# Unequal strides for the activation tiles of a float32 decoder trunk on one core

## The chip, the cores and the metric

The kernel runs on one core of a Trainium2 chip. The metric is the device time of one execution in microseconds, the median of several runs. One execution is profiled by the hardware profiler; its rows are what this text reads. Engines are named as in the profile: PE is TensorE (PEld its weight loads), DVE VectorE, ACT ScalarE, POOL GpSimd, SP SyncE.

## What is computed

A decoder trunk of two layers on 512 tokens of width 1024, in float32. Each layer adds half a SwiGLU, a mixer and another half SwiGLU, each on an RMSNorm of x:

```
h = _rmsnorm(x, ffn_pre_norm[l])
x = x + 0.5 * _swiglu(h, ffn_pre_w_gate[l], ffn_pre_w_up[l], ffn_pre_w_down[l])
h = _rmsnorm(x, mix_norm[l])
x = x + mixer(h)          # layer 0: retention | dilated attention; layer 1: gated linear attention
h = _rmsnorm(x, ffn_post_norm[l])
x = x + 0.5 * _swiglu(h, ffn_post_w_gate[l], ffn_post_w_up[l], ffn_post_w_down[l])
...
def _swiglu(h, wg, wu, wd):
    return (jax.nn.silu(h @ wg) * (h @ wu)) @ wd
```

The hidden width of the SwiGLU is 2816 = 22 x 128. A final RMSNorm ends the trunk.

## The kernel before

x stands transposed in SBUF, as eight tiles of 128 features x 512 tokens. Every float32 product is made of three products of halves (mm3, L121 to L126): a tensor is split into hi, a copy in fp32r, and lo, the rest. `mm3` multiplies hi weights by hi activations (L124), hi weights by lo activations (L125) and lo weights by hi activations (L126), all into the same PSUM bank. In each the weight slice, 128 x 128, is the stationary operand and the activation tile, 128 x 512, the moving one. In proj_n_steps (L249) it is the other way round: slices of the normed tile are stationary and the weights move.

**The normed tiles.** scaled (L165) makes xgh on ACT and xgl on DVE from x[k] and a gain, eight of each, from the pool xg with eight buffers for each tag (2048 bytes per partition and buffer). They are read by all projections of a stage; the row scale of the norm is applied to the products later.

**The SwiGLU tiles.** ffn (L292) computes 22 tiles of silu(gate) * up; halves (L112) splits each into acth and actl, from a pool with 22 buffers for each. For gate and up, 44 projections of 8 x 3 products run (proj_steps, L230); then eight output tiles of 22 x 3 products each (down, L330). There are four such stages, and the very last output tile is computed in two halves of 256 tokens (last_half, L338). halves also makes the tiles of cat, the mixers' outputs, which out_steps (L266) multiplies.

**The weights.** load_w (L83) loads a raw tile of up to 128 x 1024 on the SP queue and splits it on ACT (L89) and DVE (L90) into whi and wlo, four buffers of 4096 bytes each; weights (L77) keeps three tiles ahead of the one in use.

**Where tiles lie.** A pool is a stretch of the partition, opened in the order const, keep, xg, wpool, misc, and behind them the pool of the stage (ffn, even or odd). Within a pool each tag has its buffers one behind another. xg takes 16 x 2048 bytes, wpool 2 x 4096 for the raw tiles and 8 x 4096 for the halves. misc holds 14 KiB in tiles of 2048 bytes and small tiles which, with their alignment, take 448 bytes. So the ffn pool begins 448 bytes past a multiple of 512 from the weights. A weight slice is 512 bytes long, and the slices of a tile follow each other.

**The norm's row.** rows (L205) turns a column of values by token into a row in all partitions. For each of two halves DVE writes diag, a 128 x 512 tile (L215), and PE multiplies it by ones (L217), both into one PSUM bank; diag has two buffers. rows is called by stats_rows (L224) for the six norms with a weight behind them, by norm_steps (L403) for the eight heads of the mixers and by last_half for the two halves of the final norm:

```
for i in range(2):
    diag = self.t2k(self.misc, "diag", F32R, bufs=2)
    nc.vector.tensor_tensor(out=split2(diag[:, :nt * P]), ...)
    nc.tensor.matmul(ps[:, :nt * P], lhsT=self.ones_r, rhs=diag[:, :nt * P], start=i == 0, stop=i == 1)
```

**The order.** Each engine works through its instructions in a fixed order. It is planned when the program is built: of the instructions of an engine whose operands and buffers the planner expects to be ready, the one written first goes first. The steps of a norm are put off by hook (L93) to the ends of later projections, or to two places within a down tile; in the mixers, fill and weave (L99, L107) write projections between the steps of the heads. A tile's buffer is given to the next tile of its tag when the last reader is done.

Of the kernel before, what the change touches and what calls it, by code (L numbers as in the profile page):

```python
# [13 lines left out]
F32R = mybir.dt.float32r  # L14
# [3 lines left out]
PSUM = bass.MemoryType.PSUM  # L18

P = 128  # L20
T = 512
# [8 lines left out]
HELD = 4  # L30
PASS3 = 0.65
DOWN_SPLIT = ((0, 8), (8, 15), (15, 22))

# [12 lines left out]
class Trunk:  # L46
# [15 lines left out]
    @contextmanager  # L62
    def banks(self, **tags):
        """The PSUM banks of a phase, by purpose."""
        with self.tc.tile_pool(name=self.uid("ps"), bufs=1, space=PSUM, reuse_waits="tile") as self.ps:
            self.tags = tags
            yield
# [7 lines left out]

# [1 line left out]
    def weights(self):  # L77
        """The next weights of the plan, in halves."""
        while self.plan and len(self.ready) <= LOOK:
            self.ready.append(self.load_w(*self.plan.pop(0)))  # L80
        return self.ready.pop(0)
# [11 lines left out]
    def hook(self):  # L93
        """One of the steps put off, if any."""
        if self.pending:
            with self.tc.issue_after(self.last):
                self.pending.pop(0)()

    def fill(self, filler, us):  # L99
        """Of the filler, about this much work for the tensor engine."""  # L100
        while us > 0:
            t = next(filler, None)
            if t is None:
                return
            us -= t
# [4 lines left out]

# [1 line left out]
    def halves(self, pool, tag, src, bufs):  # L112
        """src (an SBUF or PSUM tile) as two parts of 12 significant bits each."""
        nc = self.nc
        hi = self.t2k(pool, tag + "h", F32R, bufs)
        lo = self.t2k(pool, tag + "l", F32R, bufs)
        nc.scalar.copy(out=hi, in_=src)  # L117
        nc.vector.tensor_tensor(out=lo, in0=src, in1=hi.bitcast(F32), op=ALU.subtract)  # L118
        return hi, lo

    def mm3(self, out, w, x, first, last):  # L121
        """out += w.T @ x with (hi, lo) pairs."""
        mm = self.nc.tensor.matmul
        mm(out, lhsT=w[0], rhs=x[0], start=first, stop=False)  # L124
        mm(out, lhsT=w[0], rhs=x[1], start=False, stop=False)  # L125
        self.last = mm(out, lhsT=w[1], rhs=x[0], start=False, stop=last).ins  # L126

# [1 line left out]
    def setup(self):  # L129
# [33 lines left out]

# [1 line left out]
    def scaled(self, k, idx):  # L165
        """gain * x[k] in halves."""
        nc = self.nc
        g = self.gain[:, idx * KD + k: idx * KD + k + 1]
        hi = self.t2k(self.xg, "xgh", F32R)
        lo = self.t2k(self.xg, "xgl", F32R)  # L170
        nc.scalar.activation(out=hi, in_=self.x[k], func=AF.Copy, scale=g)
        nc.vector.scalar_tensor_tensor(out=lo, in0=self.x[k], scalar=g, in1=hi.bitcast(F32), op0=ALU.mult, op1=ALU.subtract)
        if k == 0:
            self.h = []
        self.h.append((hi, lo))

    def prep(self, k, idx):
        """From x[k]: gain * x in halves, and the squares into their sum."""
        self.scaled(k, idx)
        self.squares(k)  # L180
# [13 lines left out]
    def rstd_cols(self, cols, parts, n, out, nt=NT):  # L194
        """cols: PSUM [P, nt]; sums over the partitions of parts, by token; out = (mean + eps)^-0.5."""
        nc = self.nc
        for t in range(nt):
            for i, p in enumerate(parts):
                nc.tensor.matmul(cols[:, t:t + 1], lhsT=p[:, t * P:(t + 1) * P], rhs=self.ones[:, 0:1],  # L199
                                 start=i == 0, stop=i == len(parts) - 1)  # L200
        v = self.t2k(self.misc, "var", bufs=2, shape=[P, NT])
        nc.vector.tensor_scalar(out=v[:, :nt], in0=cols[:, 0:nt], scalar1=1.0 / n, scalar2=EPS, op0=ALU.mult, op1=ALU.add)
        nc.gpsimd.tensor_tensor(out=out[:, :nt], in0=v[:, :nt], in1=self.mhalf[:, 0:nt], op=ALU.pow)

    def rows(self, cols, tag, nt=NT):  # L205
        """[P, nt] values by token -> PSUM [P, nt * P], the same row in every partition, by exact halves."""
        nc = self.nc
        ps = self.psum(tag)
        half = self.t2k(self.misc, "colh", F32R, bufs=2, shape=[P, 2, NT])
        ident = self.ident.unsqueeze(1).broadcast_to([P, nt, P])  # L210
        nc.vector.tensor_copy(out=half[:, 0, :nt], in_=cols[:, :nt])
        nc.vector.tensor_tensor(out=half[:, 1, :nt], in0=cols[:, :nt], in1=half[:, 0, :nt].bitcast(F32), op=ALU.subtract)
        for i in range(2):
            diag = self.t2k(self.misc, "diag", F32R, bufs=2)
            nc.vector.tensor_tensor(out=split2(diag[:, :nt * P]), in0=ident, in1=half[:, i, :nt].bitcast(F32).unsqueeze(2).broadcast_to([P, nt, P]),  # L215
                                    op=ALU.mult)
            nc.tensor.matmul(ps[:, :nt * P], lhsT=self.ones_r, rhs=diag[:, :nt * P], start=i == 0, stop=i == 1)  # L217
        return ps
# [9 lines left out]

# [1 line left out]
    def proj_steps(self, done):  # L230
        """One 128-wide tile of outputs, transposed: PSUM [outputs, tokens], before the row scale."""
        w = self.weights()
        ps = self.psum("pj")
        for k in range(KD):
            s = slice(k * P, (k + 1) * P)
            self.mm3(ps, (w[0][:, s], w[1][:, s]), self.h[k], k == 0, k == KD - 1)
            if k < KD - 1:
                yield PASS3
        done(ps)
        yield PASS3  # L240
# [8 lines left out]
    def proj_n_steps(self, tags, done):  # L249
        """512 outputs, tokens on partitions: 4 PSUM tiles, before the row scale."""  # L250
        ps = [self.psum(t) for t in tags]
# [14 lines left out]
    def out_steps(self, order, early, tags, idx):  # L266
        """The mixer's output projection; the first tiles wait with the last of cat."""
        nc = self.nc
# [21 lines left out]

# [1 line left out]
    def ffn(self, nxt):  # L292
        nc, tc = self.nc, self.tc
        with tc.tile_pool(name=self.uid("ffn"), bufs=KF, reuse_waits="tile") as pool, self.banks(pj=6, sc=2):
            act, held = [], []

            def glu(g, u):
# [5 lines left out]
                nc.vector.tensor_tensor(out=us, in0=us, in1=gs, op=ALU.mult)  # L303
                act.append(self.halves(pool, "act", us, KF))

# [32 lines left out]
    def last_half(self, d, ws, act, ts):  # L338
        """The end of the trunk for half of the tokens: the last tile of x, the final norm, the output."""
        nc = self.nc  # L340
# [25 lines left out]

# [1 line left out]
    def rotate(self, pool, ps, cos, sin, out, shift):  # L368
        """out = ps * cos + (ps with its rotary halves exchanged) * sin."""
        nc = self.nc  # L370
# [19 lines left out]
    def centered(self, pool, ps, t, width):  # L390
        """v * rstd less its mean over each head's width, from one PSUM tile of proj_n."""
        nc = self.nc
# [10 lines left out]
    def norm_steps(self, pool, outs, gates, cat, sq_tag, sq_bufs):  # L403
        """outs: PSUM tiles [e, tokens] of one head, with zero mean over e; cat: their index in cat."""
        nc = self.nc
# [174 lines left out]
    def retention(self, pool, qk, v, gates, need, more):  # L580
        """Emits all but the end of the last head's norm, which it returns."""
        nc = self.nc
# [37 lines left out]

# [1 line left out]
    def mixer_odd(self, nxt):  # L622
# [3 lines left out]
        with tc.tile_pool(name="odd", bufs=1, reuse_waits="tile") as pool, self.banks(pj=3, sc=3, o=2):  # L626
# [26 lines left out]
            def cums(h):  # L653
# [6 lines left out]
                nc.scalar.activation(out=e2, in_=b, func=AF.Exp, scale=-1.0)  # L660
                # In the place of the column that is exp(0), the first half's decay came.
                mid, end = slice(P // 2 - 1, T, P), slice(P - 1, T, P)
# [45 lines left out]
    def gla(self, pool, h, q, k, v, ex, tri, gates):  # L708
# [8 lines left out]
        for c in range(NT):  # L717
            nc.tensor.matmul(sc[:, sl[c]], lhsT=k[:, sl[c]], rhs=q[:, sl[c]], start=True, stop=True)
        # Of the upper right quarter of each block nothing is read: its exponents may be out of range.
        st = self.t2k(pool, "st", bufs=2)  # L720
# [72 lines left out]
def constants():  # L793
    """Tables that follow from the shapes alone."""
    f32 = np.float32
# [33 lines left out]
def layout(x, ffn_pre_norm, ffn_pre_w_gate, ffn_pre_w_up, ffn_pre_w_down, mix_norm, ab_w_in, ab_w_out, gla_w_in, gla_w_a2,  # L829
           gla_b_a, gla_w_out, ffn_post_norm, ffn_post_w_gate, ffn_post_w_up, ffn_post_w_down, final_norm):  # L830
    def tiles(w):
        """[K, N] -> [N/128, 128 (K within), K/128 * 128 (N within)]"""
        k, n = w.shape
        return w.reshape(k // P, P, n // P, P).transpose(2, 1, 0, 3).reshape(n // P, P, k)

    def wide(w):
        """[1024, 512] -> [4, 128 (K within), 2 * 512]"""
        return w.reshape(KD // 2, 2, P, T).transpose(0, 2, 1, 3).reshape(KD // 2, P, 2 * T)
# [39 lines left out]
```

## Time and profile before

| | |
|---|---|
| Runs, us | 1982.97 (median), 1982.41, 1985.41 |
| Profiled execution, first to last instruction, us | 1979.8 |
| PE busy | 1962.6 us, 99% |
| DVE, ACT, POOL busy | 45%, 31%, 5% |
| HBM read | 179.89 MB, 92 GB/s over the span |

The page gives the profiled execution by its span; a run's time also holds what lies around the span. The busy time of PE is the sum of its records; a record goes from the start of a product to its modelled end, and the next product starts before that. The time from one product's start to the next is read from the timeline, whose first column is the start in microseconds from the span's begin.

### The profile page before, as it was taken

How to read it: one execution, taken by the hardware profiler on the slowest of the kernel's cores; microseconds unless marked ns; L12 is line 12 of the kernel's file. 1: busy time of each engine (PE TensorE's matmuls, PEld its weight loads, DVE VectorE, ACT ScalarE, POOL GpSimd, SP SyncE). 2: the span in 40 equal slices, each digit the busy share in tenths (PEclk: the TensorE clock that was granted, in tenths of full speed). 3: DMA queues.
4: the chain of work that ended last, by engine and by line, in shares of the span. 5: the costliest groups of instructions: out<-in, count | busy, mean ns of one | idle time of the engine just before them, and what ended most of it. 6: DMA issues, size and time to landing. Idle time of an engine off the chain costs nothing.

```text
span 1979.8 us, 21475 instructions
## 1 busy us (share of the span) xinstructions
PE 1962.6 (99%) x8822; PEld 1593.8 (81%) x8822; DVE 900.2 (45%) x1238; ACT 611.9 (31%) x813; POOL 96.7 (5%) x69
## 2 busy tenths in 40 slices
PE   8999999999999999999999999999999999999998
PEld 7888888877777888888888888888788888888887
DVE  6444433444565544443334444333456564444323
ACT  5332222233332332222223323222424243323221
POOL 1000001100001200000110000011000020000010
PEclk9999999999999999999999999999999999999999
DMA  5333222421121322333332323323222133322222
GB/s 172 96 96 96 94 97 89 139 77 63 54 70 49 117 96 96 96 95 97 95 98 96 96 96 96 92 95 101 92 78 72 54 117 96 96 96 95 97 88 72
DMA packets 54548, 183.38 MB, mean 93 GB/s; under 512 B 6177, under 2 KB 8481, under 8 KB 54450
## 3 DMA queue, kind: packets, MB, share of 16 engines
q1 hardware_dynamic: 51408, 177.76, 28.0%
q10 hardware_dynamic: 3042, 4.26, 0.7%
q8 instruction: 69, 1.13, 0.2%
q14 instruction: 29, 0.24, 0.0%
HBM read 179.89 MB, written 2.10 MB: 92 GB/s over the span
## 4 chain that ended last, share of the span: by engine, by line
PE 98%; issue 0%; DVE 0%; DMA 0%; POOL 0%; ACT 0%; POOLq 0%; DVEq 0%; SPq 0%
PE pj L124 31%; PE pj L126 30%; PE pj L125 30%; PE sc L519 1%; PE o L547 1%; PE sc L199 1%; PE sc L594 0%; PE tp L535 0%; PE sc L217 0%; PE o L751 0%; PE o L744 0%; PE sc L733 0%; DMA wraw<-in_w_gu 0%; PE tp L603 0%; PE o L124 0%
## 5 line engine op out<-in xcount | busy, mean ns | idle before, releaser
L89 ACT CAST whi<-wraw 128x1024 fp32r<-128x1024 f32 (+1 forms) x341 | 352.0, 1033 | 1125.8 <-PE pj L125 669.0
L124 PE MATMUL pj<-xgh,whi 128*128 128x512 f32 x1704 | 677.6, 398 | 6.9 <-ACT whi L89 6.9
L126 PE MATMUL pj<-xgh,wlo 128*128 128x512 f32 x1704 | 664.9, 390 | 0.0
L125 PE MATMUL pj<-xgl,whi 128*128 128x512 f32 x1704 | 664.7, 390 | 0.0
L90 DVE TENSOR_TENSOR wlo<-wraw,whi 128x1024 fp32r<-128x1024 f32 (+1 forms) x341 | 413.1, 1212 | 306.1 <-ACT whi L89 305.0
L124 PEld LDWEIGHTS pj<-xgh,whi 128*128 128x128 f32 x1704 | 320.6, 188 | 83.5 <-issue 12.1
L126 PEld LDWEIGHTS pj<-xgh,wlo 128*128 128x128 f32 x1704 | 320.4, 188 | 67.9 <-DVE wlo L90 0.8
L125 PEld LDWEIGHTS pj<-xgl,whi 128*128 128x128 f32 x1704 | 320.9, 188 | 63.9 <-issue 1.0
L124 PE MATMUL pj<-acth,whi 128*128 128x512 f32 (+1 forms) x726 | 281.0, 387 | 0.0
L126 PE MATMUL pj<-acth,wlo 128*128 128x512 f32 (+1 forms) x726 | 280.9, 387 | 0.0
L125 PE MATMUL pj<-actl,whi 128*128 128x512 f32 (+1 forms) x726 | 280.9, 387 | 0.0
L302 DVE TENSOR_TENSOR us<-pj,rrow 128x512 f32<-128x512 f32 x88 | 60.8, 691 | 272.3 <-PE pj L126 272.3
L126 PEld LDWEIGHTS pj<-acth,wlo 128*128 128x128 f32 x726 | 135.8, 187 | 31.8
L125 PEld LDWEIGHTS pj<-actl,whi 128*128 128x128 f32 x726 | 135.8, 187 | 31.6
L124 PEld LDWEIGHTS pj<-acth,whi 128*128 128x128 f32 x726 | 135.8, 187 | 31.5
L189 POOL TENSOR_TENSOR sqa<-sqa,sq 128x512 f32<-128x512 f32 x41 | 70.6, 1722 | 1426.7 <-issue 798.1
L300 DVE TENSOR_TENSOR gs<-pj,rrow 128x512 f32<-128x512 f32 x88 | 60.8, 691 | 173.7 <-PE pj L126 173.7
L117 ACT CAST acth<-us 128x512 fp32r<-128x512 f32 x88 | 55.0, 625 | 61.1 <-DVE us L303 61.1
L303 DVE TENSOR_TENSOR us<-us,gs 128x512 f32<-128x512 f32 x88 | 60.9, 693 | 9.4 <-ACT gs L301 0.8
L325 DVE SCALAR_TENSOR_TENSOR x<-pj,x 128x512 f32<-128x512 f32 x31 | 21.5, 693 | 93.0 <-PE pj L126 93.0
L118 DVE TENSOR_TENSOR actl<-us,acth 128x512 fp32r<-128x512 f32 x88 | 60.4, 686 | 4.9 <-ACT acth L117 4.8
L301 ACT ACTIVATE gs<-gs 128x512 f32<-128x512 f32 x88 | 55.3, 630 | 4.2 <-DVE gs L300 4.2
(164 smaller groups left out, 1172.2 us busy)
## 6 DMA issues: line engine op xcount, KB each, us to landing
wraw<-in_w_gu SPq DMA_DIRECT2D x176, 512.0 KB, 3.4
wraw<-in_w_down SPq DMA_DIRECT2D x64, 448.0 KB, 3.2
wraw<-in_w_down SPq DMA_DIRECT2D x32, 512.0 KB, 3.4
wraw<-in_w_dqk SPq DMA_DIRECT2D x8, 512.0 KB, 3.4
wraw<-in_w_rqk SPq DMA_DIRECT2D x8, 512.0 KB, 3.4
wraw<-in_w_eo SPq DMA_DIRECT2D x8, 512.0 KB, 3.6
wraw<-in_w_gr SPq DMA_DIRECT2D x8, 512.0 KB, 3.4
wraw<-in_w_gv SPq DMA_DIRECT2D x8, 512.0 KB, 3.4
```

The source lines that it names most:

```text
L89: self.halved = nc.scalar.copy(out=hi[:, :cols], in_=raw[:, :cols]).ins
L90: nc.vector.tensor_tensor(out=lo[:, :cols], in0=raw[:, :cols], in1=hi[:, :cols].bitcast(F32), op=ALU.subtract)
L117: nc.scalar.copy(out=hi, in_=src)
L118: nc.vector.tensor_tensor(out=lo, in0=src, in1=hi.bitcast(F32), op=ALU.subtract)
L124: mm(out, lhsT=w[0], rhs=x[0], start=first, stop=False)
L125: mm(out, lhsT=w[0], rhs=x[1], start=False, stop=False)
L126: self.last = mm(out, lhsT=w[1], rhs=x[0], start=False, stop=last).ins
L189: nc.gpsimd.tensor_tensor(out=self.sqacc, in0=self.sqacc, in1=sq, op=ALU.add)
L300: nc.vector.tensor_tensor(out=gs, in0=g, in1=self.rrow, op=ALU.mult)
L301: nc.scalar.activation(out=gs, in_=gs, func=AF.Silu)
L302: nc.vector.tensor_tensor(out=us, in0=u, in1=self.rrow, op=ALU.mult)
L303: nc.vector.tensor_tensor(out=us, in0=us, in1=gs, op=ALU.mult)
```

## The change

The tiles of xgh and xgl get 16 elements (64 bytes) more than they use, the acth and actl tiles 8 elements (32 bytes); the tiles of cat, made by the same helper, get none. The used part is the first 512 elements, as before. diag has one buffer in place of two. The removed comments and docstrings are left out here.

```diff
+XG_STEP, ACT_STEP = 16, 8
...
-    def halves(self, pool, tag, src, bufs):
+    def halves(self, pool, tag, src, bufs, step=0):
         nc = self.nc
-        hi = self.t2k(pool, tag + "h", F32R, bufs)
-        lo = self.t2k(pool, tag + "l", F32R, bufs)
+        hi = self.t2k(pool, tag + "h", F32R, bufs, shape=[P, T + step])[:, :T]
+        lo = self.t2k(pool, tag + "l", F32R, bufs, shape=[P, T + step])[:, :T]
...
     def scaled(self, k, idx):
-        hi = self.t2k(self.xg, "xgh", F32R)
-        lo = self.t2k(self.xg, "xgl", F32R)
+        hi = self.t2k(self.xg, "xgh", F32R, shape=[P, T + XG_STEP])[:, :T]
+        lo = self.t2k(self.xg, "xgl", F32R, shape=[P, T + XG_STEP])[:, :T]
...
     def rows(self, cols, tag, nt=NT):
-            diag = self.t2k(self.misc, "diag", F32R, bufs=2)
+            diag = self.t2k(self.misc, "diag", F32R, bufs=1)
...
     def ffn(self, nxt):
-                act.append(self.halves(pool, "act", us, KF))
+                act.append(self.halves(pool, "act", us, KF, ACT_STEP))
```

## Rows read from the trace of the kernel before

**Rows 1.** The page: PE's busy time, the chain by engine.

```profile
PE 1962.6 (99%) x8822; PEld 1593.8 (81%) x8822; DVE 900.2 (45%) x1238; ACT 611.9 (31%) x813; POOL 96.7 (5%) x69
...
PE 98%; issue 0%; DVE 0%; DMA 0%; POOL 0%; ACT 0%; POOLq 0%; DVEq 0%; SPq 0%
```

**Rows 2.** Groups by line and shape: count | busy us, mean ns | idle before.

```profile
L124 PE MATMUL pj<-xgh,whi 128*128 128x512 f32 x1704 | 677.6, 398 | 6.9 <-ACT whi L89 6.9
...
L124 PE MATMUL pj<-acth,whi 128*128 128x512 f32 x682 | 268.7, 394 | 0.0
...
L124 PE MATMUL pj<-whi,xgh 128*128 128x512 f32 x112 | 45.3, 404 | 0.0
```

**Rows 3.** Two windows, tiles pj: length, busy us (count) by engine, clock, DMA.

```profile
100.00:238.00 138.00, 138.00 (x611) 114.30 (x610) 17.30 (x25) 0.00 (x0) 1.00 0.31 96
262.00:358.00 96.00, 96.00 (x413) 76.93 (x412) 4.15 (x6) 0.00 (x0) 1.00 0.30 96
```

**Rows 4.** Timeline of PE, gate and up: start, duration; 24 intervals lie between.

```profile
100.08 0.39 PE L124 MATMUL pj<-xgh,whi 128*128 128x512 f32 x1
...
105.52 0.39 PE L124 MATMUL pj<-xgh,whi 128*128 128x512 f32 x1
```

**Rows 5.** Timeline of PE, down: 24 intervals lie between.

```profile
300.06 0.39 PE L124 MATMUL pj<-acth,whi 128*128 128x512 f32 x1
...
305.66 0.39 PE L124 MATMUL pj<-acth,whi 128*128 128x512 f32 x1
```

**Rows 6.** Timeline of PE, two stretches of nine intervals on the normed tiles.

```profile
12.07 0.40 PE L126 MATMUL pj<-xgh,wlo 128*128 128x512 f32 x1
...
12.54 0.40 PE L125 MATMUL pj<-xgl,whi 128*128 128x512 f32 x1
12.78 0.39 PE L126 MATMUL pj<-xgh,wlo 128*128 128x512 f32 x1
13.00 0.39 PE L124 MATMUL pj<-xgh,whi 128*128 128x512 f32 x1
...
14.16 0.39 PE L126 MATMUL pj<-xgh,wlo 128*128 128x512 f32 x1
...
380.15 0.39 PE L125 MATMUL pj<-xgl,whi 128*128 128x512 f32 x1
...
382.23 0.39 PE L125 MATMUL pj<-xgl,whi 128*128 128x512 f32 x1
```

**Rows 7.** Timeline of PE, output projections: 47 intervals (first mixer), 51 (second).

```profile
644.83 0.39 PE L125 MATMUL pj<-catl,whi 128*128 128x512 f32 x1
...
655.79 0.40 PE L124 MATMUL pj<-cath,whi 128*128 128x512 f32 x1
...
1591.03 0.39 PE L124 MATMUL pj<-cath,whi 128*128 128x512 f32 x1
...
1602.88 0.39 PE L124 MATMUL sc<-cath,whi 128*128 128x512 f32 x1
```

**Rows 8.** Timeline of one call of rows (L205), DVE and PE.

```profile
382.54 1.29 DVE L215 TENSOR_TENSOR diag<-ident,colh 128x512 fp32r<-128x512 f32 x2
...
385.41 0.63 PE L217 MATMUL sc<-diag,ones_r 128*128 128x512 f32 x2
```

**Rows 9.** Timeline of a call in the retention, DVE and PE.

```profile
602.69 1.28 DVE L215 TENSOR_TENSOR diag<-ident,colh 128x512 fp32r<-128x512 f32 x2
...
603.43 0.50 PE L217 MATMUL sc<-diag,ones_r 128*128 128x512 f32 x1 [0.25 <-DVE diag L215]
603.77 0.59 PE L594 MATMUL sc<-qk,qk 128*128 128x256 f32 x2
604.03 0.57 PE L217 MATMUL sc<-diag,ones_r 128*128 128x512 f32 x1
```

**Rows 10.** Timeline of the last call, its products and the step behind them.

```profile
1972.84 0.92 PE L217 MATMUL sc<-diag,ones_r 128*128 128x256 f32 x2 [1.76 <-DVE diag L215]
1973.80 3.22 DVE L357 SCALAR_TENSOR_TENSOR x<-x,gain,sc 128x256 f32<-128x256 f32 x8 [0.68 <-PE sc L217]
```

## The prediction

> **What bounds the kernel now.** I read the page first: TensorE is busy in 99% of the span, and 98% of the chain that ended last is PE [rows 1]. VectorE and ScalarE are less than half busy, and no queue holds the end. So the time is the number of TensorE products times the interval from one start to the next, and the groups by shape count them [rows 2]. Products of 128x512 that touch a normed-activation tile (xgh, xgl) come 1704 and, with the weights moving, 112 times on each of three lines: 1816 x 3 = 5448 (48 more, in another bank, are left aside). Those that read a SwiGLU tile (acth, actl) come 682 x 3 = 2046. The 390 to 400 ns of one record overlap the next one, so they are no price; the price is the interval, and the timeline of PE gives it.
>
> In the first gate-and-up stage, 24 intervals take 105.52 - 100.08 = 5.44 us, **226.7 ns** each [rows 4]. In the first down stage, 24 take 305.66 - 300.06 = 5.60 us, **233.3 ns** each [rows 5]. [...] Shape, clock and number of columns are the same in both, and no wait stands between the products. What differs is where the moving tile lies. xg and wpool hold only tiles of 2048 and 4096 bytes, so every normed tile starts at the same address modulo 512 as every 512-byte slice of weights: distance 0. The small tiles of misc push the ffn pool 448 bytes on, so every SwiGLU tile lies at distance 448.
>
> Two further readings bear on what other distances cost. Near the start of the first stage, nine intervals on the same normed tiles, still at distance 0, take 14.16 - 12.07 = 2.09 us, 232.2 ns each; after a short foreign product, nine take 382.23 - 380.15 = 2.08 us, 231.1 ns [rows 6]. Single ones there are 0.22 to 0.24 us long. So 226.7 ns isn't simply the price of distance 0: it is a rhythm into which a long run of equal products falls, and which an interruption breaks. The tiles of cat, at distance 448 in the first mixer, take (655.79 - 644.83)/47 = 233.2 ns, and at distance 128 in the second (1602.88 - 1591.03)/51 = 232.4 ns [rows 7]; these never fall to 226.7.
>
> **The change, part by part.** Nothing is computed, moved or issued more: the instructions, the DMAs and their queues stay as they are. Three things differ.
>
> *The normed tiles* get a stride of 2112 bytes. The eight hi tiles stand at distances 0, 64, ... 448, the lo tiles (16896 = 33 x 512 bytes later) at the same eight. A projection walks k, three products to a tile, so no distance lasts longer than three products, where the low rhythm of the stage before lasts for a thousand. I take it that the rhythm is lost. The price is then the unsettled level for 0 and 256 (231.7, mean of rows 6), the cat level for 128 and 384 (232.4) and the level of distance 448 for the four odd multiples of 64 (233.3, the nearest that the trace has): (2 x 231.7 + 2 x 232.4 + 4 x 233.3)/8 = 232.7 ns, 6.0 more than 226.7. The four gate-and-up stages have 4 x 44 x 24 = 4224 such products: 25.3 us. The other 1224 stand in the mixers, among foreign products that already break the rhythm; half of 6.0 there makes 3.7 us. Together **+29.0 us**. The ends: at the best all go as the 0.22 us intervals of rows 6 (5448 x -6.7 ns = -37 us), at the worst as the 0.24 us ones (+72 us). I stay with the means, since over nine intervals the short and the long ones have always evened out.
>
> *The SwiGLU tiles* get 2080 bytes: 22 hi tiles at 448 + 32j modulo 512, and the lo tiles, 22 x 2080 bytes on, 192 further. Four of sixteen distances are multiples of 128 and priced as above, the rest at 233.3: 233.0 on the mean, so 2046 x -0.3 = **-0.6 us**. The ends by the same 0.22 and 0.24 us: -27 and +14 us.
>
> *One diag buffer in place of two* is the part that the name of the change leaves out. rows() (L205) is called 16 times: six for the norms, eight for the heads, two at the end. Now the second diag may be written only when the first product has read the buffer. Now the two DVE instructions end 1.6 us before PE comes to them, and the products follow each other in 0.23 us [rows 8]. With one buffer the distance between them is the first product (0.40), the hand-over to DVE (0.04: the last products end at 1973.76, DVE starts at 1973.80 [rows 10]), a diag (0.69) and the hand-over back (about 0.06, 603.97 to 604.03 [rows 9]): 1.19 us, 0.95 more. If PE stood idle for that each time, it would be **some 14 us**. But PE's order is planned: where the second diag is expected late, other ready products are put between, as the two of L594 between the two of L217 at 603.43 [rows 9]. Next to 14 of the calls there are projections or output products that wait for nothing. Behind the very last call nothing is left: there one diag of 0.42 us and the hand-overs come on the path, 0.6 us. With about 1 us for places filled badly I take **+1.5 us** between the ends 0 and 14. DVE stands still between the first diag and the first product, up to 2 us longer than now; the splits of weights behind it (L90) run three tiles of 5.4 us ahead of their use, so TensorE sees nothing of that. In norm_steps the next DVE instruction (L420) waits for the second product anyway.
>
> The sum is 29.0 - 0.6 + 1.5 = +29.9 us. The profiled execution spans 1979.8 us, and the median of the runs, 1982.97, is 3.2 us longer by what lies around the span; that stays. 1983.0 + 29.9 = **2012.9 us**.
>
> **The rivals.** (1) *Distance has no part in it.* The two levels come from something else in which the groups differ: the normed tiles lie below the weights, the SwiGLU and cat tiles above them. For it: both cat stretches, at different distances, lie near 233 [rows 7]. Against it: the unsettled level is as high at unchanged places [rows 6]. Both tile groups keep their intervals, and only the diag is paid: 1983.0 + 1.5 = 1984.5 us, within 0.2%. [...]
>
> (2) *The low rhythm survives, and the SwiGLU tiles join it.* It is on the other side. If 226.7 ns is where products settle unless a bad distance holds them off, a mixture that meets 448 in only a few tiles would settle too. Place: the down stages. Price: 2046 x (226.7 - 233.3) = -13.5 us, with the diag 1971 us. It decides as long as the normed tiles lose less than 12.0 us / 5448 = 2.2 ns each. For it: the low level is the commonest of all. Against it: cat at 128 doesn't settle in 51 intervals [rows 7].
>
> (3) *The diag waits come on the path*, on top of the forecast: 14 in place of 1.5, 1983.0 + 29.0 - 0.6 + 14 = 2025 us. For it: PE runs in its order and can't pass a waiting product. Against it: the filled gap of rows 9.
>
> **How the numbers follow.** The forecast gets 0.64, rival 3 0.08, rival 1 0.14, rival 2 0.14. The forecast's own spread is a level of 230.7 to 234.7 ns, 2003 to 2022 us (4.0 and 8.0 ns in place of 6.0). The range runs from rival 1 to rival 3: 1983 to 2026 us (rounded outward); the ends that every single product would have to pay, and rival 2, are what it leaves out. About 0.2%, 4 us, is what a measurement of this kernel can tell from no change. Slower has the forecast and rival 3, 0.72; the same has rival 1, 0.14; faster has rival 2, 0.14.
>
> **What would show it.** In the profile after, the interval of the gate-and-up stages shall be 231 to 234 ns, with single ones of 0.22 to 0.24 us mixed, and the stage of 1056 products some 6 us longer; the down stages shall stay at 232 to 234 ns. Between the two L217 of a call other products of PE shall stand, and a PE wait for diag of over 0.5 us shall appear at the end alone. I am wrong if a gate-and-up stage still steps at 226.7 ns (rival 1 or 2), if it steps at less than 224, or if PE waits for diag add up to over 5 us.

## The result and the profile after

The changed kernel takes **2004.07 us** (median of 4 runs, 2003.87 to 2004.24) against 1982.9 us before (1982.41 to 1985.41): a ratio of 1.0107, 95% interval 1.0092 to 1.0121. It is slower, by 21 us by the medians and by 2002.3 - 1979.8 = 22.5 us by the spans of the two profiled executions. Lines after L31 have moved down by one.

The page of the kernel after: span, busy time, chain by engine.

```profile
span 2002.3 us, 21471 instructions
...
PE 1983.8 (99%) x8822; PEld 1595.2 (80%) x8822; DVE 900.7 (45%) x1238; ACT 611.4 (31%) x813; POOL 97.5 (5%) x69
...
PE 98%; DVE 0%; issue 0%; DMA 0%; POOL 0%; ACT 0%; POOLq 0%; DVEq 0%; SPq 0%
```

The same 8822 products stand on PE as before [rows 1], and PE is still the whole chain. So the products follow each other more slowly. The two windows of [rows 3], of the kernel after:

```profile
100.00:238.00 138.00, 138.00 (x598) 112.00 (x598) 17.30 (x25) 0.00 (x0) 1.00 0.29 93
262.00:358.00 96.00, 96.00 (x417) 77.76 (x416) 4.15 (x6) 0.00 (x0) 1.00 0.31 96
```

598 products in place of 611 fit into the gate-and-up window, 417 in place of 413 into the down window, at the same granted clock of 1.00. The timeline of PE shows the new interval; 24 lie between these two rows, as in [rows 4]:

```profile
100.06 0.40 PE L125 MATMUL pj<-xgh,whi 128*128 128x512 f32 x1
...
105.60 0.40 PE L125 MATMUL pj<-xgh,whi 128*128 128x512 f32 x1
```

5.54/24 = 230.8 ns in place of 226.7. With every interval of the trace put to the product that begins it, the 22.5 us are: normed tiles +22.6 (1292.2 against 1269.6), SwiGLU tiles -3.5 (473.9 against 477.4), diag +1.7, cat +1.5, the two halves at the end +0.6, the rest -0.4.

The single diag buffer shows in the call at 1043 us, first PE and then DVE (compare [rows 8]):

```profile
1043.02 0.39 PE L218 MATMUL sc<-diag,ones_r 128*128 128x512 f32 x1
1043.25 0.39 PE L125 MATMUL pj<-xgh,whi 128*128 128x512 f32 x1
...
1043.95 0.39 PE L125 MATMUL pj<-xgh,whi 128*128 128x512 f32 x1
1044.20 0.50 PE L218 MATMUL sc<-diag,ones_r 128*128 128x512 f32 x1
...
1043.45 0.69 DVE L216 TENSOR_TENSOR diag<-ident,colh 128x512 fp32r<-128x512 f32 x1 [2.52 <-PE sc L218]
```

DVE waits 2.52 us for the first product; PE puts four others between the two and reaches the second 1.18 us after the first, without a gap. In the other calls but the last, too, four to twelve products stand between the two, and PE waits before none of the second ones. At the very end nothing is left to put between (compare [rows 10]):

```profile
1994.85 0.39 PE L218 MATMUL sc<-diag,ones_r 128*128 128x256 f32 x1 [1.76 <-DVE diag L216]
1995.27 0.42 DVE L216 TENSOR_TENSOR diag<-ident,colh 128x256 fp32r<-128x256 f32 x1 [0.48 <-PE sc L218]
...
1995.75 0.46 PE L218 MATMUL sc<-diag,ones_r 128*128 128x256 f32 x1 [0.52 <-DVE diag L216]
1996.25 3.22 DVE L358 SCALAR_TENSOR_TENSOR x<-x,gain,sc 128x256 f32<-128x256 f32 x8 [0.56 <-PE sc L218]
```

### The profile page after: what moved, and what is told of

It is laid out like the page before. It is cut to its first block, busy times and chain, and to the rows that moved or that the text cites. A ratio compares the mean times of both kernels' runs of the same rounds, so it can differ in the third digit from the quotient of the medians.

```text
span 2002.3 us, 21471 instructions
## 1 busy us (share of the span) xinstructions
PE 1983.8 (99%) x8822; PEld 1595.2 (80%) x8822; DVE 900.7 (45%) x1238; ACT 611.4 (31%) x813; POOL 97.5 (5%) x69
## 4 chain that ended last, share of the span: by engine, by line
PE 98%; DVE 0%; issue 0%; DMA 0%; POOL 0%; ACT 0%; POOLq 0%; DVEq 0%; SPq 0%
PE pj L125 31%; PE pj L127 31%; PE pj L126 30%; PE sc L520 1%; PE o L548 1%; PE sc L200 1%; PE sc L218 0%; PE sc L595 0%; PE tp L536 0%; PE o L752 0%; PE o L745 0%; PE sc L734 0%; DMA wraw<-in_w_gu 0%; PE tp L604 0%; PE o L127 0%
## 5 line engine op out<-in xcount | busy, mean ns | idle before, releaser
L125 PE MATMUL pj<-xgh,whi 128*128 128x512 f32 x1704 | 685.8, 402 | 6.7 <-ACT whi L90 6.7
L127 PE MATMUL pj<-xgh,wlo 128*128 128x512 f32 x1704 | 672.5, 395 | 0.0
```

## The experiments

My theory: the interval depends on the distance between the moving tile and the weights, and on what went before, so that a distance held over a stage settles at a level of its own. Rivals: the place of a tile decides and not its distance; any distance settles if it is held, and only a mixture costs. All kernels start from the one before. A time given as "one execution" was run once, beside runs of the kernel before.

**Each part alone.** First the diag buffer:

```diff
-            diag = self.t2k(self.misc, "diag", F32R, bufs=2)
+            diag = self.t2k(self.misc, "diag", F32R, bufs=1)
```

> The kernel before with one diag buffer and nothing else. My theory: the planner puts other products between the two of a call, so the span grows from 1979.8 us by 1 to 3 us, with a PE wait for diag of over 0.5 us at the very end alone; the gate-and-up stages still step at 226.7 ns and the down stages at 233.3 ns. Rival (the diag waits come on the path): 10 us or more, in PE waits for diag of 0.9 us each.

One execution: 1988.2 us, span 1986.3, 6.5 us more than before. The stages step as expected (611 and 413 products in the two windows). What I had not expected lies in the second mixer. Windows there of the kernel with one diag buffer (granted clock: third column from the right):

```profile
1403.50:1407.00 3.50, 3.50 (x10) 1.51 (x9) 1.92 (x2) 2.82 (x5) 0.00 (x0) 1.00 0.00 0
1407.00:1410.50 3.50, 3.50 (x8) 2.02 (x7) 0.00 (x0) 2.80 (x4) 0.00 (x0) 0.52 0.44 150
1410.50:1414.00 3.50, 3.50 (x9) 2.73 (x9) 0.00 (x0) 3.47 (x3) 0.00 (x0) 0.51 0.00 0
```

The same stretch of the kernel before:

```profile
1407.00:1410.50 3.50, 3.50 (x17) 2.85 (x16) 0.00 (x0) 3.47 (x3) 0.00 (x0) 1.00 0.29 118
1410.50:1414.00 3.50, 3.50 (x17) 2.92 (x16) 0.11 (x1) 3.47 (x4) 0.00 (x0) 1.00 0.00 0
```

In this execution the granted clock stood at a low level, 0.52 and 0.51, for some 7 us; in the second of the two windows PE has 9 products where the kernel before has 17 at 1.00. That costs about half of the 7 us, 3.4 us; in the profiled executions of before and after the clock stayed at 1.00 there. So this execution can't price the diag, and I ran the same kernel again, ten times:

> Once more the kernel before with one diag buffer and nothing else, for its price without a fall of the clock in the second mixer. From the stages of the first look I expect 3 us: a span of 1983 us, a ratio of 1.0015. Rival (the whole 6.5 us of the first look belongs to the diag): 1.003.

1987.03 us (1986.47 to 1988.38, 10 runs), ratio 1.0025, interval 1.0016 to 1.0035. Its profiled execution spans 1984.5 us and holds 3.4 us at the low level (1.7 us): without it 1982.8, 3.0 us more than before, as I expected; the first execution gives 1986.3 - 3.4 - 1979.8 = 3.1. The two executions of this kernel differ by 3.4 us of low clock and by 1.8 us of span. The runs say 4.6 us: the ratio I had expected, 1.0015, lies just outside the interval, and the rival's, 1.003, inside. Part of the rest goes with the clock: the mean granted clock of these runs is 0.9970, that of the runs of before beside them 0.9975, and 0.0005 of 1985 us is some 1 us, an estimate from figures of three digits (at a granted clock of 0.5 about half of the time is lost, as the 9 products in place of 17 show, and that is what the mean falls short by). Whether one diag buffer is what makes the clock fall more often or longer, the runs don't settle. The waits of PE say where part of the 3.0 us is. The kernel with one diag buffer (first execution; waited for: us, times, longest):

```profile
PE sc L217 <- DVE diag L215: 3.3, 4, 1.8
PE pj L124 <- ACT cath L117: 1.5, 1, 1.5
```

The kernel before:

```profile
PE sc L217 <- DVE diag L215: 2.7, 3, 1.8
...
PE pj L124 <- ACT cath L117: 0.5, 1, 0.5
```

0.6 us more of waiting for diag, at the end; and 1.0 us in the second mixer, where the last head's row comes later, so its cat comes later, and the output projection waits for it. The changed kernel shows the same two sums, 3.3 and 1.5 us.

The stride of the normed tiles, with one diag buffer since the room is needed:

```diff
-        hi = self.t2k(self.xg, "xgh", F32R)
-        lo = self.t2k(self.xg, "xgl", F32R)
+        hi = self.t2k(self.xg, "xgh", F32R, shape=[P, T + 16])[:, :T]
+        lo = self.t2k(self.xg, "xgl", F32R, shape=[P, T + 16])[:, :T]
```

> The wide stride of the normed tiles and one diag buffer; the SwiGLU tiles as before. My theory (a run of one distance settles into a low rhythm, a mixture doesn't): gate and up step at 231 to 231.5 ns as with the whole change, the down stages stay at 233.3 ns, and the span is 3.5 us (2046 x 1.7 ns) longer than with the whole change: some 2005.8 us. Rival (place alone, distance has no part): gate and up at 226.7 ns, 1981 to 1983 us.

One execution: 2007.4 us, span 2005.5. The two windows of this kernel:

```profile
100.00:238.00 138.00, 138.00 (x598) 112.04 (x597) 17.30 (x25) 0.00 (x0) 1.00 0.29 95
262.00:358.00 96.00, 96.00 (x414) 77.32 (x413) 4.15 (x6) 0.00 (x0) 1.00 0.30 96
```

598 as with the whole change, 414 as before: the loss is all here. The stride of the SwiGLU tiles alone (`halves` as in the change, ACT_STEP 8, two diag buffers):

> The wide stride of the SwiGLU tiles alone; two diag buffers. My theory: the down stages step at 231.6 ns in place of 233.3, gate and up at 226.7 ns: 2046 x -1.7 ns = -3.5 us, a span of 1976.3 us. Rival (a mixture is always worse than one distance held): the down stages at 233.3 ns or above, 1979.8 us or more.

One execution: 1981.51 us, span 1979.6, in which the granted clock was 0.5 for some 3.4 us of the second mixer (1.7 us). The down window of this kernel:

```profile
262.00:358.00 96.00, 96.00 (x416) 77.66 (x415) 4.15 (x6) 0.00 (x0) 1.00 0.30 96
```

Its 2046 SwiGLU products take 474.5 us, 2.9 less than before. The span as it stands is all but the rival's 1979.8 us; without the 1.7 us of the clock it is 1977.9, between that and my 1976.3. The products are my theory's, at 231.9 ns where I had said 231.6.

**A distance held.** An unused tile shifts all that lies behind it; every stride stays 2048. 64 bytes in misc bring the SwiGLU tiles from distance 448 to 0:

```diff
         nc.vector.memset(self.mhalf, -0.5)
+        nc.vector.memset(self.misc.tile([P, 16], F32, name="shift", tag="shift", bufs=1), 0.0)
```

> The kernel before with one unused tile of 64 bytes in misc, so that all SwiGLU tiles lie at distance 0 in place of 448, still with one stride of 2048. My theory (distance decides, and distance 0 held for long settles): the down stages step at 226.7 ns like the normed tiles, 2046 x -6.7 ns = -13.6 us, and cat of the first mixer, now at distance 0 too, gains up to 1 us: a span of 1965 to 1967 us, some 1969 us in all. Rival (place decides: tiles above the weights step at 233.3 ns whatever the distance): 1979.8 us, no change.

**1970.48 us** (1969.67 to 1970.7, 4 runs), ratio 0.9937, interval 0.9921 to 0.9954. The down window of this kernel:

```profile
262.00:358.00 96.00, 96.00 (x425) 79.47 (x425) 4.84 (x7) 0.00 (x0) 1.00 0.30 96
```

425 products in place of 413: 226.7 ns, 463.8 us for the 2046, 13.6 less, as expected. The profiled execution, 1968.5 us, again holds 7 us at the low clock; without the 3.4 us that they cost it is 1965.1, where I had said 1965 to 1967. That tiles above the weights step at 233.3 ns whatever their distance is ruled out: what lies behind the unused tile is 64 bytes further up, and that is all. The next kernels change the distance of both groups. A tile of 64, 256, 384 or 320 bytes at the head of wpool moves the weights and what lies behind them; the normed tiles stay where they were. All further spans hold 3.4 or 7 us of low clock in the second mixer (1.7 or 3.4 us of time); the windows shown lie outside it.

```diff
         nc.vector.memset(self.ones, 1.0)
+        nc.vector.memset(self.wpool.tile([P, 16], F32, name="apart", tag="apart", bufs=1), 0.0)
...
         nc.vector.memset(self.mhalf, -0.5)
+        nc.vector.memset(self.misc.tile([P, 32], F32, name="shift", tag="shift", bufs=1), 0.0)
```

> All strides 2048 as before, two diag buffers; an unused tile of 64 bytes ahead of the weights and one of 128 bytes in misc put every normed tile at distance 448 and every SwiGLU tile at distance 64. My theory (a distance held over a whole stage settles into a level of its own, which depends on the distance): gate and up step at 233.3 ns, as the SwiGLU tiles did at 448; the down stages step at one level, without a value from me beyond 226 to 234 ns. Span 1996 to 2012 us. Rival (only the mixture costs; any distance held falls to the low level): gate and up at 226.7 ns, 1980 us or less.

One execution: 2005.63 us, span 2003.7. Its two windows:

```profile
100.00:238.00 138.00, 138.00 (x593) 110.72 (x592) 16.98 (x25) 0.00 (x0) 1.00 0.29 92
262.00:358.00 96.00, 96.00 (x421) 78.81 (x420) 4.15 (x6) 0.00 (x0) 1.00 0.31 96
```

> As before, with 256 bytes ahead of the weights and 320 in misc: normed and SwiGLU tiles all at distance 256. My theory says that both groups step at the same level, since only the distance counts; if the pattern repeats every 256 bytes it is 226.7 ns for both (span 1965 to 1968 us), if it doesn't, it is 231 to 234 ns for both (1995 us or more). Rival (the groups differ by more than the distance): two different levels.

One execution: 1969.77 us, span 1967.8:

```profile
100.00:238.00 138.00, 138.00 (x610) 114.31 (x609) 17.29 (x25) 0.00 (x0) 1.00 0.31 95
262.00:358.00 96.00, 96.00 (x426) 79.50 (x425) 4.84 (x7) 0.00 (x0) 1.00 0.31 96
```

> As before, with 384 bytes ahead of the weights and 192 in misc: normed and SwiGLU tiles all at distance 128. My theory: both groups step at the same level, 232 to 232.5 ns as cat did at 128, single ones between 0.228 and 0.241 us; gate and up 5.5 ns longer than before, down 1 ns shorter: a span of 2003 to 2007 us. Rival (any distance held falls to the low level): 226.7 ns for both, 1965 to 1968 us.

One execution: 2011.83 us, span 2009.9, above what I expected:

```profile
100.00:238.00 138.00, 138.00 (x595) 111.91 (x594) 17.25 (x25) 0.00 (x0) 1.00 0.30 92
262.00:358.00 96.00, 96.00 (x415) 77.84 (x414) 4.15 (x6) 0.00 (x0) 1.00 0.31 95
```

The third gate-and-up stage of this execution and the third down stage step more slowly:

```profile
1100.00:1238.00 138.00, 138.00 (x593) 111.04 (x592) 16.79 (x25) 0.00 (x0) 1.00 0.30 96
1290.00:1386.00 96.00, 96.00 (x413) 77.23 (x412) 4.15 (x6) 0.00 (x0) 1.00 0.31 96
```

So 128 held has two levels: 232.4 ns in the first and the last stage of each kind, 233.3 in the two between, where I had expected one of 232 to 232.5. What decides between them, no run shows.

> All strides 2048, two diag buffers; 320 unused bytes ahead of the weights and 96 in misc: normed tiles held at distance 192, SwiGLU tiles held at 32. If the pattern repeats every 256 bytes, gate and up step as at 448, at 233.1 to 233.3 ns. The down stages take a level between those of 0 and 64, 226.7 to 228.9 ns, if the level rises steadily with the distance: a span of 2000 to 2004 us. Rival (the pattern repeats only every 512 bytes): gate and up at some other level.

One execution: 2015.67 us, span 2013.7:

```profile
100.00:238.00 138.00, 138.00 (x593) 111.17 (x592) 17.13 (x25) 0.00 (x0) 1.00 0.29 92
262.00:358.00 96.00, 96.00 (x413) 77.10 (x412) 4.16 (x6) 0.00 (x0) 1.00 0.31 92
```

So the normed tiles lose the low level as soon as they are *held* at 448, 192 or 128 (593 to 595 products, 233.3 ns over the third gate-and-up stage of each; means over a stage leave out the few intervals beside a foreign product), and keep it at 256 (226.7 ns). "Any distance held settles low" is false; that each settles at one level of its own holds but for 128. The normed tiles themselves never moved here, so no place of theirs decides. Nor does the weights' alone: in the kernel before, the same weights go with 226.7 ns on the normed tiles and 233.3 on the SwiGLU tiles. The distance between the two fits every run, though none moved both together. 0 and 256 agree, as if the pattern repeated every 256 bytes; 192 and 448 agree too, but 32 and 128 also reach 233.3 ns, so that this pair says little. The level doesn't rise steadily: 32 costs the SwiGLU tiles 233.3 ns, 64 only 228.9. There my expectation failed.

**A mixture.** Hi tiles 256 bytes wider (`shape=[P, T + 64]` for xgh alone), one diag buffer: distances 0 and 256 in turn.

> The hi tiles of the normed activations get 256 spare bytes each (distances 0 and 256 in turn), the lo tiles none; one diag buffer, SwiGLU tiles as before. If the pattern repeats every 256 bytes, as the held distances 0 and 256 suggest, this mixture is none for the engine: gate and up at 226.7 ns, a span of 1983 us (with the diag's 3.1 us), plus 1.6 or 3.2 us where the clock falls in the second mixer. Rival (every change of distance or of stride breaks the low rhythm): 231 ns, some 2003 us.

One execution: 1987.35 us, span 1985.4 with 3.4 us at the low clock, so 1983.7 without. The gate-and-up window:

```profile
100.00:238.00 138.00, 138.00 (x611) 114.26 (x610) 17.29 (x25) 0.00 (x0) 1.00 0.30 95
```

611, as before: neither the wider stride nor the alternation of these two costs anything. Hi and lo tiles 128 bytes wider (`T + 32`):

> The normed tiles get 128 spare bytes each: distances 0, 128, 256, 384 in turn, hi and lo; one diag buffer, SwiGLU tiles as before. Theory of memory (an interval depends on its distance and on what went before; distance 0 is cheap only when held): gate and up at 231 to 232 ns, a span of 2002 to 2007 us. Rival (each product pays the level of its own distance as if held, 226.7 for 0 and 256, 232.8 for 128 and 384): the mean of the two, 229.7 ns, a span of some 1997 us.

One execution: 2014.72 us, span 2012.8, of which 3.4 us are the clock's. The gate-and-up window:

```profile
100.00:238.00 138.00, 138.00 (x596) 111.43 (x595) 17.30 (x25) 0.00 (x0) 1.00 0.29 92
```

232.2 ns over the third gate-and-up stage: beyond both expectations, and on the side of memory. The rival's mean of the levels held would be (226.7 + 233.3)/2 = 230.0. By distance, means over the third gate-and-up stage (for 64 held, the down stages), in ns:

| distance | held | in the change | in steps of 128 |
|---|---|---|---|
| 0 | 226.7 | 232.7 | 234.6 |
| 64 | 228.9 | 228.9 | |
| 128 | 233.3 | 230.0 | 230.6 |
| 192 | 233.3 | 232.8 | |
| 256 | 226.7 | 232.8 | 232.2 |
| 320 | | 229.1 | |
| 384 | | 230.1 | 231.3 |
| 448 | 233.3 | 232.8 | |

The program gives a tag's first buffer first and then the others from the last back, so a projection of the changed kernel meets 0, 448, 384 and so on down to 64. Held, 0 and 256 are the cheapest. In the changed kernel, where they come right after three products at 64 and 320, they cost as much as 192 and 448; in steps of 128, 0 is the dearest. Two distances that differ by 256 cost the same within 0.2 ns in the change, but 0 and 256 differ by 2.4 ns in the steps of 128: the repeat every 256 bytes does not hold there.

**A faster kernel.** 64 bytes in misc as above, and 320 in the pool of the second mixer, so that cat lies at distance 0 in both mixers too:

```diff
             nc.vector.memset(low, 1.0)
+            nc.vector.memset(pool.tile([P, 80], F32, name="shift2", tag="shift2"), 0.0)
```

> As before, with 64 bytes in misc and 320 in the pool of the second mixer: the normed tiles, the SwiGLU tiles and the tiles of cat in both mixers all at distance 0. My theory: the run with 64 bytes alone stood at 1970.5 us; cat of the second mixer goes from 232 to 230 ns as that of the first did, 192 products by some 2 ns or 0.4 us: 1969.5 to 1970.5 us. Rival (cat lies among waits, and its interval doesn't count): 1970.5 us, no difference to that run.

**1969.47 us** (1968.28 to 1970.51, 5 runs), ratio 0.9936, interval 0.9922 to 0.9949: it beats the kernel before and the changed one. The intervals put to cat add up to 91.4 us, 0.9 less than with the 64 bytes alone; the two runs' ranges overlap, so the runs don't tell the two apart.

## Why the prediction was right, and where it was off

*The bound and the price* held: the time is PE's interval, and the change acts on it. That distance has a part in it (against rival 1) is shown by 64 unused bytes that bring 12 us. The same product takes 226.7 or 233.3 ns by where the moving tile starts against the weights (distance 0 or 448); what in the hardware makes the difference, no run here shows.

*The normed tiles* were the term that was mis-sized: +29.0 us said, +22.6 measured. "I take it that the rhythm is lost" was right of this mixture: it has 231.1 ns in a gate-and-up stage, and 0 and 256 lost their low level. The reason given was only half right. That no distance lasts longer than three products is not what loses it, since 0 and 256 in turn keep 226.7 ns; it is lost by meeting the other distances, and at 448, 192 and 128 it isn't there even when they are held. The step that was off is the price by distance, 232.7 on the mean. I put the level of 448 (233.3) to all four odd multiples of 64; 192 and 448 cost 232.8, but 64 and 320 cost 229. 128 and 384 cost 230 in the mixture, not 232.4. 0 and 256 cost 232.8, not 231.7. The four gate-and-up stages grew by 19.5 us where I had 25.3, the mixers' share by 3.1 where I had 3.7.

*The SwiGLU tiles*: -0.6 said, -3.5 measured, 231.6 ns in place of 233.0 and thus below the 232 to 234 ns that I had named as a sign, for the same reason: sixteen distances priced from four levels. Rival 2, that they would fall to 226.7, needed other distances: with the 64 bytes, held at 0, they do exactly that, mixed they don't.

*The diag buffer*: 1.19 us between the two products said, 1.18 measured, with four other products between, no gap and thus no 14 us (rival 3). The last call went from 0.38 to 0.90 us, 0.5 where I had 0.6; the 0.38 fell into a stretch at a granted clock of 0.50 (from 1971.2 us on), the 0.90 into one at 1.00 (up to 1995.9 us), so that this pair isn't taken at one clock. The sum was 1.5 said, 3.0 by the profile and 4.6 by the runs: I had named no one who waits for a head's row, and the output projection of the second mixer does, for 1.0 us more. Some 1 us of the rest goes with the clock, by the estimate above; what else makes it up was not found.

The sum of 2012.9 us lies 8.8 us over the result, and the largest part of it are the 6.4 us of the normed tiles. The direction rested on the one reading that the low rhythm of the normed tiles doesn't outlast the mixture, and the runs bear that out for these distances. That a change of distance by itself breaks the rhythm they don't: for a mixture of 0 and 256 the same reasoning would have failed, and no row of before told the two cases apart. To that extent it was luck which distances the change happens to meet.

## What to carry to other kernels

Where PE is the whole chain, read the interval from start to start of each kind of product; two levels for one shape (here 226.7 and 233.3 ns) are a lead. Before spreading addresses, shift them: one unused tile of 64 bytes moves a whole group and tells in a single run what a distance is worth. Here the gain lay in giving every group the distance that was already the best, and spreading them took it away.

## What was not expected

The level that a held distance settles at isn't steady over the distances: 226.7 ns at 0 and again at 256, 233.3 at 32, 228.9 at 64, 232.4 or 233.3 at 128, 233.3 at 192. A distance that is cheap when held is among the dearest in a mixture (226.7 against 232.7 ns at 0), so an average over held levels doesn't price one.

The clock fell in the second mixer, between 1393 and 1428 us, in eleven of the fourteen profiled executions, all but those of before, of the whole change and of the normed tiles' stride: to a granted clock of 0.5, for 3.4 or 7 us. Ahead of it PE worked through the eight float32 products of L644 (L645 in some of the kernels; 1403.96 to 1408.00 us in the first execution with one diag buffer) while ACT ran its functions; so it did in the three executions without a fall (1403.06 to 1406.69 us in that of before). At 1.7 or 3.4 us it is as large as the effects of the smaller parts, so a single execution must be read with its clock. What decides in which executions it falls was not tried, nor were other orders of the distances, or hi and lo tiles held at different ones.
